# One list of other work for all heads of the attention, and new planning figures

## The chip, the cores and the metric

One core of one Trainium2 chip runs the kernel. The metric is the device time of one execution in microseconds (us). Before the change three runs took 1665.37 to 1666.42 us, the median is 1666.23 us. One further execution was profiled.

## The reference

A block of two branches over a sequence of 1024 tokens of 1024 channels, all in float32:

```python
h = rmsnorm(x, norm_g); proj = h @ w_in      # split in 12 parts
# branch a: mLSTM in both directions, 4 heads of 256, y_a
dq = apply_rope(b_q, positions); dk = apply_rope(b_k, positions)   # 8 heads x 2 x 64
p = softmax(q . k * scale)                   # for both halves j = 0, 1 of a head
att = (p[:, :, 0] - lam * p[:, :, 1]) @ v    # v: 8 heads of 128
y_b = rmsnorm(att, subln_g) * (1 - lambda_init) * silu(b_z)
mix = sigmoid(g_a + gb[0]) * (y_a @ w_branch_a) + sigmoid(g_b + gb[1]) * (y_b @ w_branch_b)
out = rmsnorm(x + mix @ w_out, final_g)
```

The change lies in branch b, the differential attention.

## The kernel before

**Precision.** Every float32 product is made of three matmuls on operands split in a high and a low part (`H` and `L` in the tile names), so each 128-deep step of a projection is three matmuls.

**Stages.** The kernel runs, in this order: norm and transposition of x; most projections of branch a in a form that saves products; the attention of branch b (the stage that the change touches); the mLSTM of branch a; the products with the branch weights and with w_out. Projections that the attention itself needs, or that fill its gaps, run inside the attention stage.

**One head of the attention** works on eight tiles t of 128 rows of q, in units that `da_parts` (L1168) makes:

- S(t): the scores of a tile, both halves of the head, into two PSUM tiles of 128 x 1024 (12 matmuls, L1185). VectorE takes the maximum of each (`nm`, L1188), ScalarE the exponential (`e`, L1190), and VectorE joins both (L1196).
- T(t, g): eight transpositions of the joined tile in two groups of four (L160), each group in a PSUM tile with the tag "T". ScalarE copies it to `pH` (L1209), VectorE makes the low part `pL` (L1210). There are two such PSUM tiles.
- PV(t2, g): the products with v for two tiles t, in two units of 12 matmuls (L1221); ScalarE copies the result to `att` (L1223).
- M(t2): transposition of `att` and the sums of squares of it (L1233); the last one of a head starts the root on GpSimd.
- G(half): scaling, and the store of y_b for a half of the sequence.

`da_cycle` (L1270) puts these into one order per tile: in even tiles S and T of the tile before, then M; in odd tiles S and PV, then T; in tiles 4 and 5 also G of the head before. T, M and G of a head's last tiles fall into the first tiles of the next head.

**The other work** is woven between: rotated q and k of a later head (`da_proj`: four times eight pieces of three matmuls of 512 columns, then the rotation on VectorE and GpSimd and a DMA into place), z of a head (two times eight pieces), v of two heads (`da_v`: 32 pieces of six matmuls of 256 columns, L675), and gates of the final mix (`gate_units`, 16 pieces, taken by `fill(m)`). The even heads in `R_EARLY` have q and k made in an earlier stage and only load them (`load_qk`), and the heads in `Z_EARLY` load z; these units have cost 0. All pieces of `proj` have the line L653.

**The planner.** `Weaver` (L70) sets the order of the matmul engine before anything runs. Each unit has a cost in us (multiples of `MM` and `TP`), names of units after which it may come, each with a lag, and maybe a PSUM tag whose tiles are held for a time after the unit (`LAG`: T tiles 2.9, S 5.0). `weave` takes several lists. A list falls into lanes, each kept in order. At each step the unit goes first that can start first by these figures, and among equals the one whose place in its list, as a share of the list's cost, is lowest:

```python
best = min(heads, key=lambda l: (max(self.ready(l[0][1]), self.now), l[0][0]))
```

A `Chain` is a run of units that is put as a whole once none of them has to wait. The order is kept on the matmul engine; the order on the other engines is made from it later. Weights of a piece are loaded by `run` (L610) up to two keys ahead, on the queue of SyncE, which also carries the loads of q, k and z and the stores of y_b.

**The order before.** `build` weaves head by head: the units of head h with a list of other work for that head, so that each head's list is spread over that head alone. Even heads have a rotated q/k projection and z (48 pieces), odd heads v (32 pieces), head 0 the last 12 pieces of v of heads 0 and 1, a projection and a gate unit, and head 7 a gate unit and z. The units of v for heads 2n and 2n+1 come after the last PV of head 2n-2, which stands in tile 1 of head 2n-1; the halves of z come after G of the head before plus 6.0 us.

Of the kernel before, what the change touches and what calls it, by code (L numbers as in the profile page):

```python
# [13 lines left out]

S = 1024
D = 1024
EPS = 1e-6
NH_A, DH = 4, 256
NH_B = 8
# [15 lines left out]


INF = 1.0e9
FILL = (1, 0, 0, 0, 0, 0, 0, 1)
Z_EARLY = (0, 1, 3, 5)
R_EARLY = (0, 2, 4, 6)  # L40
MM = 0.214
TP = 0.109

LAG = dict(Th=2.9, Sh=5.0, PVh=2.9, Mh=2.0, qk=14.0, T=6.8, PV=3.0, M=1.5, F=6.0, TTh=1.9, TT=3.2, POh=1.6,
# [85 lines left out]
class Block:  # L130
# [529 lines left out]
    def v_units(self, seg, n, done, after=(), order=(0, 1, 2, 3)):  # L660

        box = {}

        def piece(s2, g):
            if g == 0:
                box["ps"] = self.psA.tile([128, 2, 256], F32, name="pj", tag="pj", bufs=2)
            ps = box["ps"]
            i, kh, k0 = g // 4, (g // 2) % 2, 2 * (g % 2)
            wH, wL = (wide(x) for x in self.wt[(seg, n, kh)])
            s = 2 * s2 + i  # L670
            c = slice((s % 4) * 128, (s % 4) * 128 + 128)
            for k in range(k0, k0 + 2):
                hH, hL = (x[s // 4][:, 4 * kh + k, c] for x in (self.hH, self.hL))
                for m, (l, r) in enumerate(((hH, wH), (hL, wH), (hH, wL))):
                    self.t.matmul(ps[:, i, :], lhsT=l, rhs=r[:, k, :], start=(kh == 0 and k == 0 and m == 0),  # L675
                                  stop=(kh == 1 and k == 3 and m == 2))
            if g == 7:
                done(s2, ps)

        return [Unit(6 * TP, lambda s2=s2, g=g: piece(s2, g), ((seg, n, (g // 2) % 2),), after=after)  # L680
                for s2 in order for g in range(8)]

    def bank(self, tag, shape=(128, 512)):
# [397 lines left out]
    def da_proj(self, h, st):  # L1081
        A, v, a, p, q = self.A, self.v, self.a, self.p, self.q
        w1 = self.w1
        fb = lambda x: x.bitcast(F32)
        kA, kB = ("rope", h, 0), ("rope", h, 1)

        def first(half, pa):
            c = slice(half * 512, (half + 1) * 512)
            m = [w1.tile([128, 512], F32, name=f"m{i}", tag=f"m{i}", bufs=1) for i in range(2)]
            st["m"] = m  # L1090
            v.tensor_tensor(out=m[0], in0=pa, in1=self.cosT[:, c], op=ALU.mult)
            v.tensor_tensor(out=m[1], in0=pa, in1=self.sinT[:, c], op=ALU.mult)

        def second(half, pb):
            c = slice(half * 512, (half + 1) * 512)
            if half == 0:
                st["k"] = w1.tile([128, 2, S], F32R, name="kst", tag="kst", bufs=2)
            qq = st["q", half] = w1.tile([128, 2, 512], F32R, name="qq", tag="qq", bufs=3)
            m = st["m"]

            hl = w1.tile([128, 4, 512], F32R, name="hl", tag="hl", bufs=2)
            v.tensor_tensor(out=fb(hl[:, 2]), in0=pb, in1=self.sinT[:, c], op=ALU.mult)
            v.tensor_tensor(out=fb(hl[:, 3]), in0=pb, in1=self.cosT[:, c], op=ALU.mult)
            p.tensor_tensor(out=m[0], in0=m[0], in1=fb(hl[:, 2]), op=ALU.subtract)
            p.tensor_tensor(out=m[1], in0=fb(hl[:, 3]), in1=m[1], op=ALU.add)
            for i in range(2):
                p.tensor_copy(hl[:, i, :], m[i])
                p.tensor_tensor(out=hl[:, 2 + i, :], in0=m[i], in1=fb(hl[:, i, :]), op=ALU.subtract)
            for x in range(2):
                for i, to in enumerate((st["k"][:, :, c], qq)):  # L1110
                    for j in range(2):
                        r, g = 64 * j + 32 * x, 64 * (1 - i) + 32 * j
                        q.dma_start(out=fb(to[r:r + 32]), in_=fb(hl[g:g + 32, x::2]))

        kz = ("w_in", OFF["bz"] + 128 * h)

        def zz(half, ps):
            st["g", half] = g = w1.tile([128, 512], F32, name="zg", tag="zg", bufs=2)
            a.activation(out=g, in_=ps, func=AF.Tanh, scale=0.5)
            v.scalar_tensor_tensor(out=g, in0=g, scalar=1.0, in1=ps, op0=ALU.add, op1=ALU.mult)  # L1120

        def load_qk(half):
            if half == 0:
                st["k"] = w1.tile([128, 2, S], F32R, name="kst", tag="kst", bufs=2)
            st["q", half] = w1.tile([128, 2, 512], F32R, name="qq", tag="qq", bufs=3)
            for x in range(2):
                for j in range(2):
                    r, g = 64 * j + 32 * x, 32 * j
                    if half == 0:
                        q.dma_start(out=fb(st["k"][r:r + 32]), in_=self.rd[h][64 + g:96 + g, x])  # L1130
                    q.dma_start(out=fb(st["q", half][r:r + 32]), in_=self.rd[h][g:g + 32, x, :, half * 512:half * 512 + 512])

        qk = []
        if h in R_EARLY:
            qk = [Unit(0.0, lambda: load_qk(0)), Unit(0.0, lambda: load_qk(1), name=("qk", h), after=((("S", h - 1, 3), 1.0),), lane=1)]
        for half in range(0 if h in R_EARLY else 2):
            qk += self.proj(kA, half, lambda ps, half=half: first(half, ps))
            qk += self.proj(kB, half, lambda ps, half=half: second(half, ps), name=("qk", h))
        def load(half):
            t = w1.tile([128, 512], F32, name="zr", tag="zr", bufs=2)  # L1140
            q.dma_start(out=t, in_=self.zd[h][:, half * 512:(half + 1) * 512])
            zz(half, t)

        if h in Z_EARLY:
            z = [Unit(0.0, lambda half=half: load(half), name=("z", h) if half else None) for half in range(2)]
        else:
            z = self.proj(kz, 0, lambda ps: zz(0, ps)) + self.proj(kz, 1, lambda ps: zz(1, ps), name=("z", h))
        for half in range(2):
            z[(half + 1) * len(z) // 2 - 1].after = ((("G", h - 1, half), LAG["G"]),)
        return qk, z  # L1150
# [17 lines left out]
    def da_parts(self, h, st):  # L1168
# [43 lines left out]
        def pv(t2, g):  # L1212
            vH, vL = st["v"]
            if g == 0:
                st["pv"] = self.bank("T")
            ps = st["pv"]
            pH, pL = st.pop(("pT", t2, g))
            for i in range(4):
                k = 4 * g + i
                for m, (l, r) in enumerate(((vH, pH), (vH, pL), (vL, pH))):  # L1220
                    self.t.matmul(ps[:, 0:256], lhsT=l[:, k, :], rhs=r[:, i, :], start=(k == 0 and m == 0), stop=(k == 7 and m == 2))  # L1221
            if g == 1:
                a.copy(st["att"][:, t2 * 256:(t2 + 1) * 256], ps[:, 0:256])  # L1223
# [24 lines left out]
        def scale(half):  # L1248
# [3 lines left out]
            for i in range(4):  # L1252
# [3 lines left out]
            q.dma_start(out=self.yb[h][:, half * 512:(half + 1) * 512], in_=g)  # L1256

        return dict(
            S=lambda t: Unit(6 * MM, lambda: scores(t), tag="S", hold=LAG["Sh"], name=("S", h, t), after=((("qk", h), 5.0 if h in R_EARLY else LAG["qk"]),)),
            T=lambda t, g: Unit(4 * TP, lambda: transposes(t, g), tag="T", hold=LAG["Th"], name=("T", h, t, g),  # L1260
                                after=((("S", h, t), LAG["T"]),)),
            PV=lambda t2, g: Unit(12 * TP, lambda: pv(t2, g), tag="T" if g == 0 else None, hold=LAG["PVh"], name=("PV", h, t2, g),
                                  after=((("T", h, 2 * t2 + 1, g), LAG["PV"]), (("v", h // 2), 1.0))),
            M=lambda t2: Unit(2 * TP, lambda: squares(t2), tag="T", hold=LAG["Mh"], name=("M", h, t2),
                              after=((("PV", h, t2, 1), LAG["M"]), (("z", h if t2 == 3 else -1), 0.0))),
# [474 lines left out]
    def build(self):  # L1740
# [19 lines left out]
        do = lambda f, cost=0.0: Unit(cost, f)  # L1760
        pool = lambda *x, **k: tc.tile_pool(*x, **k)
        with pool(name="const", bufs=1) as self.const, \
# [112 lines left out]
            w.banks.update(S=1, T=2)  # L1875
            qk, z = zip(*[self.da_proj(h, sts[h]) for h in range(NH_B)])
            v0 = self.da_v(0, sts[0:2])
            w.add(do(lambda: setattr(self, "ahead", True)), *qk[0], *z[0], *v0[:20])
            prev = None
            for h in range(NH_B):  # L1880
                cur = self.da_parts(h, sts[h])
                main = sum((self.da_cycle(cur, prev, t) for t in range(8)), [])
                ahead = qk[h + 1] if h + 1 < NH_B else []
                if h + 1 == NH_B:
                    nxt = fill(FILL[h]) + z[h]
                elif h % 2 == 1:
                    nxt = ahead + self.da_v((h + 1) // 2, sts[h + 1:h + 3]) + fill(FILL[h])
                else:
                    nxt = z[h - 1] + ahead + fill(FILL[h]) + z[h] if h else v0[20:] + ahead + fill(FILL[0])
                w.weave(main, nxt)  # L1890
                prev = cur
            end = sum((self.da_cycle(None, prev, t) for t in range(6)), [])
            w.weave(end[:-2], fill(2))
            more, c = fill(1), self.PIECES // 2
# [85 lines left out]
```

## Time and profile before

| what | us |
|---|---|
| median of three runs | 1666.23 |
| lowest and highest run | 1665.37, 1666.42 |
| profiled execution, its own time | 1662.69 |
| span in the profile | 1660.9 |
| TensorE matmul busy | 1612.8 (97%) |
| VectorE busy | 1076.5 (65%) |
| ScalarE busy | 809.4 (49%) |
| GpSimd busy | 663.1 (40%) |

The span runs from the first to the last instruction of the core. In the profile PE is the matmul engine, PEld its weight loads, DVE VectorE, ACT ScalarE, POOL GpSimd, SP the queue of SyncE. L with a number is a line of the kernel. Tiles are named output<-inputs: S are scores, T the small PSUM tiles, pj the PSUM tiles of projections. A row of the chain of waits has the start, the length, the engine, the tile, the line and the count of instructions. Matmuls are pipelined and their ends are modelled, so a row's length is a little more than the time to the next start.

### The profile page before, as it was taken

The page shows a single profiled execution, that of the slowest core. Times are in us where ns is not written, and L with a number is a line of the kernel's source. Part 1 is how long each engine was busy: PE and PEld are TensorE (multiplying, and loading weights), DVE is VectorE, ACT ScalarE, POOL GpSimd, SP SyncE. Part 2 cuts the span into 40 slices and gives each one's busy share as a digit, 9 for nine tenths or more (in the row PEclk, how much of TensorE's full clock was granted, in tenths as well). Part 3 has the DMA queues.
Part 4 walks back from the last instruction along what each step waited for, and adds up shares of the span by engine and source line. Part 5 has one row for each costly group of instructions (what it writes and reads, how often), then busy time and mean ns, then how long its engine had stood idle before and what let it go on. Part 6 is the DMA issues. An engine that isn't in the chain of part 4 may idle for free.

```text
span 1660.9 us, 25336 instructions
## 1 busy us (share of the span) xinstructions
PE 1612.8 (97%) x9251; PEld 1357.6 (82%) x9251; DVE 1076.5 (65%) x1898; ACT 809.4 (49%) x1634; POOL 663.1 (40%) x709
## 2 busy tenths in 40 slices
PE   7999999999999999999999999999999999999998
PEld 5898778878888888797797887877888888888887
DVE  5734887686876517677768778776157867446633
ACT  6433555555544435555545555554357656442221
POOL 3744676767679722513312511521322332222000
PEclk9999999999999999999999999999999999999999
DMA  5433444444444451511401411310697863466422
GB/s 188 146 127 129 129 129 141 123 132 127 140 122 157 152 165 52 127 41 50 114 20 58 101 40 52 82 47 33 178 316 255 272 201 130 140 229 215 178 90 88
DMA packets 195854, 216.53 MB, mean 130 GB/s; under 512 B 12441, under 2 KB 143858, under 8 KB 195218
## 3 DMA queue, kind: packets, MB, share of 16 engines
q1 hardware_dynamic: 192514, 209.14, 40.8%
q10 hardware_dynamic: 3216, 5.78, 0.9%
q8 instruction: 73, 1.20, 0.3%
q14 instruction: 51, 0.42, 0.1%
HBM read 137.18 MB, written 69.30 MB: 124 GB/s over the span
## 4 chain that ended last, share of the span: by engine, by line
PE 62%; DVE 5%; ACT 4%; POOL 4%; issue 2%; DMA 1%; SPq 0%; POOLq 0%; DVEq 0%; ACTq 0%
PE pj L653 22%; PE T L401 10%; PE S L1185 5%; PE pj L675 5%; PE pj L1690 5%; PE T L160 5%; PE T L1221 5%; ACT e L1190 2%; PE I L156 2%; PE T L156 1%; DVE nm L1188 1%; PE SS L156 1%; PE PO L156 1%; POOL wH L374 1%; POOL s L351 1%
## 5 line engine op out<-in xcount | busy, mean ns | idle before, releaser
L653 PE MATMUL pj<-hH,wH 128*128 128x512 f32 x544 | 222.8, 409 | 0.1
L653 PE MATMUL pj<-hH,wL 128*128 128x512 f32 x544 | 213.9, 393 | 0.8 <-POOL wL L245 0.8
L653 PE MATMUL pj<-hL,wH 128*128 128x512 f32 x544 | 213.2, 392 | 0.6 <-DVE hL L809 0.6
L1190 ACT ACTIVATE e<-S,nm 128x1024 f32<-128x1024 f32 x128 | 142.7, 1122 | 91.0 <-DVE nm L1188 91.0
L1188 DVE TENSOR_REDUCE nm<-S 128x1 f32<-128x1024 f32 x128 | 150.7, 1219 | 46.9 <-PE S L1185 46.7
L247 POOL TENSOR_TENSOR wL<-raw,wH 128x1024 fp32r<-128x1024 f32 x27 | 68.4, 2534 | 149.8 <-ACT wH L239 137.4
L1209 ACT CAST pH<-T 128x512 fp32r<-128x512 f32 x128 | 69.9, 589 | 117.6 <-PE T L160 117.6
L401 PE MATMUL T<-TH,wL 128*128 128x512 f32 x368 | 122.2, 393 | 2.3 <-ACT u L408 2.3
L401 PE MATMUL T<-TH,wH 128*128 128x512 f32 x368 | 122.1, 391 | 0.4 <-ACT u L408 0.3
L653 PEld LDWEIGHTS pj<-hH,wL 128*128 128x128 f32 x544 | 102.1, 188 | 24.2 <-POOL wL L245 2.1
L653 PEld LDWEIGHTS pj<-hL,wH 128*128 128x128 f32 x544 | 102.6, 189 | 17.7 <-DVE hL L809 1.5
L653 PEld LDWEIGHTS pj<-hH,wH 128*128 128x128 f32 x544 | 102.5, 188 | 16.4 <-ACT hH L808 0.5
L1185 PE MATMUL S<-kst,qq 64*128 64x512 f32 x768 | 110.4, 410 | 0.9 <-ACT e L1190 0.6
L1210 DVE TENSOR_TENSOR pL<-T,pH 128x512 fp32r<-128x512 f32 x128 | 82.4, 682 | 29.0 <-ACT pH L1209 29.0
L1185 PEld LDWEIGHTS S<-kst,qq 64*128 64x128 f32 x768 | 69.1, 185 | 31.6 <-issue 12.7
L1245 POOL TENSOR_TENSOR zg<-att,zg 128x512 f32<-128x512 f32 x16 | 21.1, 1316 | 181.4 <-ACT att L1223 165.5
L1196 DVE SCALAR_TENSOR_TENSOR e<-e,r,e 128x1024 f32<-128x1024 f32 x64 | 91.6, 1431 | 2.0
L401 PE MATMUL T<-hH,wH 128*128 128x512 f32 x280 | 92.3, 390 | 0.2 <-DVE cin L578 0.2
L401 PE MATMUL T<-hH,wL 128*128 128x512 f32 x272 | 90.2, 391 | 0.7 <-DVE oz L510 0.7
L597 DVE SCALAR_TENSOR_TENSOR pj<-cin,cols,pj 128x512 f32<-128x512 f32 x128 | 87.1, 747 | 0.0
L401 PEld LDWEIGHTS T<-TH,wL 128*128 128x128 f32 x368 | 69.1, 188 | 20.3 <-ACT u L408 6.1
L401 PEld LDWEIGHTS T<-TH,wH 128*128 128x128 f32 x368 | 69.1, 188 | 15.6 <-ACT u L408 1.2
(417 smaller groups left out, 4596.6 us busy)
## 6 DMA issues: line engine op xcount, KB each, us to landing
raw<-in_w_in_dram SPq DMA_DIRECT2D x76, 512.0 KB, 4.0
rd<-rot SPq DMA_DIRECT2D x16, 512.0 KB, 3.1
x<-in_x_dram SPq DMA_DIRECT2D x8, 512.0 KB, 4.7
avH<-tz SPq DMA_DIRECT2D x16, 256.0 KB, 2.0
cak<-y SPq DMA_DIRECT2D x16, 256.0 KB, 2.7
cakH<-cin SPq DMA_DIRECT2D x16, 256.0 KB, 4.7
cakL<-tz SPq DMA_DIRECT2D x16, 256.0 KB, 4.6
gm<-oz SPq DMA_DIRECT2D x16, 256.0 KB, 2.7
```

The source lines that it names most:

```text
L156: self.t.matmul(out, lhsT=l, rhs=r, start=(i == 0), stop=(i == n - 1))
L160: self.t.transpose(out, in_, self.ident[0:k, 0:k])
L401: self.t.matmul(ps, lhsT=l[:, k, :], rhs=r[:, k, :], start=(first and k == 0 and m == 0), stop=(k == 3 and m == 2), skip_group_check=not f ...
L597: v.scalar_tensor_tensor(out=acc, in0=raw[:, o + x:o + x + 512], scalar=w(x), in1=acc, op0=ALU.mult, op1=ALU.add)
L653: self.t.matmul(ps, lhsT=l[:, k, :], rhs=r, start=(n == 0), stop=(n == 23))
L675: self.t.matmul(ps[:, i, :], lhsT=l, rhs=r[:, k, :], start=(kh == 0 and k == 0 and m == 0), stop=(kh == 1 and k == 3 and m == 2))
L1185: self.t.matmul(ps[:, o], lhsT=qq[r, x, c], rhs=k[r, y, o], start=(m == 0), stop=(m == 2))
L1188: v.tensor_reduce(out=nm, in_=ps, axis=AX.X, op=ALU.max, negate=True)
L1190: a.activation(out=e, in_=ps, func=AF.Exp, bias=nm[:, 0:1], accum_out=Z[:, j, t:t + 1])
L1196: v.scalar_tensor_tensor(out=e0, in0=e, scalar=r[:, 0:1], in1=e0, op0=ALU.mult, op1=ALU.add)
L1221: self.t.matmul(ps[:, 0:256], lhsT=l[:, k, :], rhs=r[:, i, :], start=(k == 0 and m == 0), stop=(k == 7 and m == 2))
L1690: self.t.matmul(ps, lhsT=x[:, s], rhs=y[:, c], start=(k == 0 and m == 0), stop=(k == 7 and m == 2))
```

## The change

The eight weaves become one. All heads' units stand in one main list, and all other work in one second list, which is woven against it from the first tile of head 0 to the last of head 7. All 32 pieces of v of heads 0 and 1 run before the weave (20 before). The second list has, in order: q/k of head 1, the loads of q/k of head 2, a gate unit, the loads of z of head 1; then for h = 2, 4, 6: v of heads h and h+1, q/k of head h+1, z of head h, and the loads of q/k of head h+2 and of z of head h+1 (after head 6: a gate unit and z of head 7). The order of the matmul pieces in it is that of before. The loads of z get a lane of their own, and the first load of q/k of an even head goes to the lane of the second and waits for the scores of the head two before. `FILL` is gone. The planning figures change: `MM` 0.214 to 0.227, S 6 to 7.5 `MM`, a half of PV 12 to 13 `TP`, a piece of v 6 to 6.6 `TP`. The arithmetic of the kernel is the same.

```diff
-FILL = (1, 0, 0, 0, 0, 0, 0, 1)
 Z_EARLY = (0, 1, 3, 5)
 R_EARLY = (0, 2, 4, 6)
-MM = 0.214
+MM = 0.227
 TP = 0.109
...
-        return [Unit(6 * TP, lambda s2=s2, g=g: piece(s2, g), ((seg, n, (g // 2) % 2),), after=after)
+        return [Unit(6.6 * TP, lambda s2=s2, g=g: piece(s2, g), ((seg, n, (g // 2) % 2),), after=after)
                 for s2 in order for g in range(8)]
...
         if h in R_EARLY:
-            qk = [Unit(0.0, lambda: load_qk(0)), Unit(0.0, lambda: load_qk(1), name=("qk", h), after=((("S", h - 1, 3), 1.0),), lane=1)]
+            qk = [Unit(0.0, lambda: load_qk(0), after=((("S", h - 2, 7), 1.0),), lane=1),
+                  Unit(0.0, lambda: load_qk(1), name=("qk", h), after=((("S", h - 1, 3), 1.0),), lane=1)]
...
         if h in Z_EARLY:
-            z = [Unit(0.0, lambda half=half: load(half), name=("z", h) if half else None) for half in range(2)]
+            z = [Unit(0.0, lambda half=half: load(half), name=("z", h) if half else None, lane=2) for half in range(2)]
...
-            S=lambda t: Unit(6 * MM, lambda: scores(t), tag="S", hold=LAG["Sh"], ...
+            S=lambda t: Unit(7.5 * MM, lambda: scores(t), tag="S", hold=LAG["Sh"], ...
...
-            PV=lambda t2, g: Unit(12 * TP, lambda: pv(t2, g), tag="T" if g == 0 else None, ...
+            PV=lambda t2, g: Unit(13 * TP, lambda: pv(t2, g), tag="T" if g == 0 else None, ...
...
-            w.add(do(lambda: setattr(self, "ahead", True)), *qk[0], *z[0], *v0[:20])
-            prev = None
-            for h in range(NH_B):
-                cur = self.da_parts(h, sts[h])
-                main = sum((self.da_cycle(cur, prev, t) for t in range(8)), [])
-                ahead = qk[h + 1] if h + 1 < NH_B else []
-                if h + 1 == NH_B:
-                    nxt = fill(FILL[h]) + z[h]
-                elif h % 2 == 1:
-                    nxt = ahead + self.da_v((h + 1) // 2, sts[h + 1:h + 3]) + fill(FILL[h])
-                else:
-                    nxt = z[h - 1] + ahead + fill(FILL[h]) + z[h] if h else v0[20:] + ahead + fill(FILL[0])
-                w.weave(main, nxt)
-                prev = cur
+            w.add(do(lambda: setattr(self, "ahead", True)), *qk[0], *z[0], *v0)
+            parts = [self.da_parts(h, sts[h]) for h in range(NH_B)]
+            main = sum((self.da_cycle(x, y, t) for x, y in zip(parts, [None] + parts) for t in range(8)), [])
+            prev, nxt = parts[-1], qk[1] + qk[2] + fill(1) + z[1]
+            for h in (2, 4, 6):
+                nxt += self.da_v(h // 2, sts[h:h + 2]) + qk[h + 1] + z[h] + (qk[h + 2] + z[h + 1] if h < 6 else fill(1) + z[7])
+            w.weave(main, nxt)
```

More of the change, by code (lines that the diff above doesn't have):

```diff
@@ L1258, in da_parts @@
         return dict(
-            S=lambda t: Unit(6 * MM, lambda: scores(t), tag="S", hold=LAG["Sh"], name=("S", h, t), after=((("qk", h), 5.0 if h in R_EARLY else LAG["qk"]),)),
+            S=lambda t: Unit(7.5 * MM, lambda: scores(t), tag="S", hold=LAG["Sh"], name=("S", h, t), after=((("qk", h), 5.0 if h in R_EARLY else LAG["qk"]),)),
             T=lambda t, g: Unit(4 * TP, lambda: transposes(t, g), tag="T", hold=LAG["Th"], name=("T", h, t, g),
                                 after=((("S", h, t), LAG["T"]),)),
-            PV=lambda t2, g: Unit(12 * TP, lambda: pv(t2, g), tag="T" if g == 0 else None, hold=LAG["PVh"], name=("PV", h, t2, g),
+            PV=lambda t2, g: Unit(13 * TP, lambda: pv(t2, g), tag="T" if g == 0 else None, hold=LAG["PVh"], name=("PV", h, t2, g),
                                   after=((("T", h, 2 * t2 + 1, g), LAG["PV"]), (("v", h // 2), 1.0))),
```

## The prediction

> **What bounds the kernel now.** I read the page's busy line first, then busy time by stretches of the attention stage, then the chain of waits inside single stretches.
>
> ```profile
> span 1660.9 us, 25336 instructions
> ...
> PE 1612.8 (97%) x9251; PEld 1357.6 (82%) x9251; DVE 1076.5 (65%) x1898; ACT 809.4 (49%) x1634; POOL 663.1 (40%) x709
> ```
>
> The matmul engine is busy 97% of the span, so only what it waits can be won. The change acts in the attention stage alone. Its first and last scores matmul mark it, and the longest wait of the engine there is for the pL tiles (sum, times, longest):
>
> ```profile
> L1185 PE MATMUL S<-kst,qq x768: 383/393/628, 621.2 to 1143.1; 64*128 64x512 f32 x192
> PE T L160 <- DVE pL L1210: 12.5, 7, 2.2
> ```
>
> The stage by stretches, cut where the matmul engine's idle time begins and ends (columns: length, then busy time of PE, PEld, DVE, ACT, POOL, then granted clock):
>
> ```profile
> 702.00:743.00 41.00, 41.00 (x340) 38.31 (x339) 30.03 (x43) 21.36 (x48) 6.32 (x10) 1.00 0.15 44
> 743.00:757.00 14.00, 11.63 (x85) 9.37 (x84) 11.27 (x17) 10.72 (x24) 5.70 (x5) 1.00 0.44 132
> 757.00:818.00 61.00, 61.00 (x372) 48.71 (x370) 46.22 (x63) 30.01 (x65) 23.68 (x24) 1.00 0.25 61
> 818.00:833.00 15.00, 12.21 (x82) 9.15 (x83) 12.44 (x17) 9.16 (x21) 2.98 (x4) 0.92 0.47 107
> 833.00:876.00 43.00, 43.00 (x353) 40.31 (x352) 28.57 (x42) 21.25 (x48) 6.77 (x10) 0.99 0.10 31
> 1121.00:1127.00 6.00, 3.89 (x32) 2.80 (x30) 4.86 (x8) 4.02 (x10) 0.00 (x0) 1.00 0.00 0
> ```
>
> Inside a head the engine idles not at all (41.00 of 41, 61.00 of 61, 43.00 of 43). The idle time lies at the seams around the odd heads and in tile 4 of head 7 (1121 to 1127), 2 to 3 us at a time. The chain shows why. First a stretch of head 1, filled with pieces of the v projection (six matmuls each), one tile of scores (S) to the next:
>
> ```profile
> 710.80 1.59 PE S L1185 x11
> 712.39 1.02 PE T L160 x8
> 713.41 2.86 PE pj L675 x24
> 716.27 0.22 PE T L160 x2
> 716.49 1.42 PE pj L675 x12
> 717.92 1.59 PE S L1185 x12
> 719.51 3.02 PE T L1221 x24
> 722.53 1.43 PE pj L675 x12
> 723.96 0.87 PE T L160 x8
> 724.83 1.42 PE pj L675 x12
> 726.26 1.59 PE S L1185 x12
> ```
>
> Even tile: S, transpositions, 4 pieces, squares, 2 pieces. Odd tile: S, the products with v, 2 pieces, transpositions, 2 pieces. Now head 2, filled with the three-matmul pieces of `proj`, with the starts of tiles 4, 5 and 6:
>
> ```profile
> 773.59 1.58 PE S L1185 x12
> 775.17 1.02 PE T L160 x8
> 776.20 2.75 PE pj L653 x12
> 778.95 0.22 PE T L160 x2
> 779.17 2.09 PE pj L653 x9
> 781.26 1.60 PE S L1185 x11
> ...
> 789.43 1.58 PE S L1185 x12
> ...
> 796.84 1.59 PE S L1185 x12
> ...
> 810.31 1.58 PE S L1185 x11
> ```
>
> Here the even tile has 4 + 3 pieces. And the seam before head 3, with no piece at all:
>
> ```profile
> 817.97 1.64 PE S L1185 x11
> 819.61 1.23 DVE nm L1188
> ...
> 826.22 2.26 DVE nm L1188 x2
> 828.48 0.61 DVE pL L1210
> 829.13 0.44 PE T L160 x2
> 829.57 0.76 PE S L1185 x2
> ```
>
> The squares need the PSUM bank that pL frees. VectorE comes to pL only after both maxima (2.26 us): pieces normally hide this, and here there are none.
>
> **The change part by part.** What matters is how many pieces the planner wants, and how many it has.
>
> *The planning figures.* Scores go from 1.28 to 1.70 us (measured 1.59), a `proj` piece from 0.642 to 0.681 (measured 2.09/3 = 0.70), a v piece from 0.654 to 0.719 (1.43/2 = 0.72), products with v from 1.31 to 1.42 a half (3.02/2 = 1.51). None changes an instruction; they change how many pieces the planner puts before a unit is ready by its LAG figures. Even tile: the squares need a T bank, 2.9 - 0.436 = 2.46 us after the transpositions, 4 pieces before and after. The next S is due 5.0 us after the last: 0.87 + 4 x 0.642 + 0.22 = 3.66 left 1.34, so 3 pieces; now 0.87 + 2.72 + 0.22 = 3.81 leaves 1.19, so 2. Odd tile: 2 + 2 in both. Tile 4 takes 6. In tile 5 the scale unit's bank is held 2.46 us more, so 4 + 2. A head wants 6+4+6+4+6+6+6+4 = 42 pieces; head 0, with no head before it, 8+7+7+4+6+4+6+4 = 46.
>
> *One list.* It holds four rotated q/k projections (32 pieces each), four of z (16), three of v (32) and two gate units (16): 320, or 40 a head. Demand by lags (42) lies above the share (40), so the lags place the pieces and other work runs a little ahead. One block is left: v of heads 2n and 2n+1 waits for the last products of head 2n-2, in tile 1 of an odd head. Ahead of the first block stand 32 + 16 = 48 pieces, of which head 0 takes 46; between blocks 32 + 32 + 16 = 80 against 84. So tile 0 of heads 1, 3 and 5 has 2 pieces of 6, where it had none. Gone are the empty tiles 6 and 7 of heads 1, 3 and 5, tile 7 of heads 2, 4 and 6, and tile 4 of head 7. The end of head 7 stays: z of head 7 waits for the scale units of head 6, which leaves 3 pieces in tile 6 and none in tile 7, as now.
>
> *The stage in tiles.* Two more places are needed: tile 0 of head 1 with its successor, empty of pieces, and tile 6 of head 7.
>
> ```profile
> 693.14 1.60 PE S L1185 x11
> ...
> 698.78 1.66 PE S L1185 x11
> 1136.28 1.59 PE S L1185 x11
> ```
>
> An even tile takes 781.26 - 773.59 = 7.67 now, less one piece 6.97. An odd one takes 789.43 - 781.26 = 8.17, tile 4 takes 796.84 - 789.43 = 7.41. Tile 5 takes 810.31 - 796.84 = 13.47 with 11 pieces, 10.0 without five of them; I take 10.1. A full head is 3 x 6.97 + 3 x 8.17 + 7.41 + 10.1 = 62.9. In heads 1, 3 and 5, tile 0 stays at the 698.78 - 693.14 = 5.6 of the empty one, since pL ends it and two pieces only fill part of the wait; five tiles with v pieces take 0.15 more each (717.92 - 710.80 = 7.12 against 6.97): 62.9 - 6.97 + 5.6 + 0.75 = 62.3. Head 0 starts with S (1.6), 0.85 of transpositions from tile 1 on, and 8, 7 and 7 pieces of 0.70: 7.2, 7.4 and 7.4; then come 8.17 x 3 + 6.97 x 2: 60.4. Head 7 up to its last tile: 2 x 6.97 + 2 x 8.17 + 7.41 + 10.1 + 5.0 (1143.1 - 1.8 - 1136.28) = 52.8. Sum 60.4 + 3 x 62.9 + 3 x 62.3 + 52.8 = 488.8. Now it is 1143.1 - 621.2 = 521.9, less 1.8 within the last S (1.6 and a short wait): 520.1.
>
> *v of heads 0 and 1 ahead of the loop.* The last 12 pieces move from head 0 to before the first S: 12 x 0.72 = 8.6 us, the same on both sides, as the engine has no gap there. So the stage wins 520.1 - 488.8 - 8.6 = 22.7.
>
> *Lanes and loads.* The first half of q and k of an even head (four DMAs for k, four for q) is now held until the scores of the head two before are done; its buffers are free only then, so nothing becomes later. The z loads of heads 1, 3 and 5 (one DMA, one tanh, one VectorE operation per half) get a lane of their own and come up to half a head earlier. I cost both at nothing: inside a head VectorE is busy 46.22 of 61 us, 76%, and shorter heads take that to some 80%. Without that cover they would stand ahead of a pL: two operations on 128x512 as pL is, 0.61 each by its row, for two halves of three heads 7 us at most.
>
> *What the rows can't show.* All engines but the matmul engine are put in a new order around the new places. From below it costs nothing (the v stretches run with these piece counts and idle 0). From above it is the first rival's 15.9. I take 4.7, near the lower end because those rows are nearest: some 0.6 us a head. So 22.7 - 4.7 = 18 us.
>
> The profiled execution took 1662.7 us, a span of 1660.9 and 1.8 around it, and goes to 1644.7. The median of the runs, 1666.2, lies 3.5 above it; the same step gives **1648**.
>
> The seam at 818 to 833 has a granted clock of 0.92, about 1.2 us; the other stretches have 0.99 or 1.00. I leave it in both sums. The Trainium skill (TensorE: Matmul & The Clock Gate, "HAM oscillation — how this bites in real kernels") says that an idle gap over some 3.4 us throttles the array; by that rule the shorter seams would win this 1.2 us too.
>
> **The rivals.**
>
> *Ten pieces are too few between `proj` pieces.* They are a little shorter than v pieces, and the even tile now leaves S 0.7 us less. If the old 7.67 us are needed, each of some 23 even tiles outside the v stretches waits 0.69: 15.9 us, a gain of 22.7 - 15.9 = 6.8, 1659. For it: VectorE is the next busiest. Against: v stretches have 7.12 (717.92 - 710.80) and idle 0.
>
> *The seams can't be filled.* If the waits on pL come from two T banks and not from missing pieces, they only move with the seams: no change, 1666. Against: the same two banks idle 0 in every body. The Trainium skill (Perfetto Trace Analysis, "Optimization Strategy") speaks for it: a gap that repeats can mean too few PSUM buffers. By it the gaps would be found between the seams too, and the trace has none there.
>
> *Shares decide after all*, 40 pieces a head without the lag's excess: tile 0 of heads 1, 3 and 5 is then full. Its 5.6 us hold 6.97 - 4 x 0.69 = 4.2 of work now, so 3 x 1.4 come back, and the 4.7: 1648 - 8.9 = 1639.
>
> *Slower: a weight late behind the load queue.*
>
> ```profile
> SPq L1131 <- PE S L1185: 75.2, 3, 28.6
> ```
>
> The queue stands up to 28.6 us at the loads of q, which wait for scores. Today the seam lies between the end of v and the next rotated projection; now it follows at once. Its second weight is needed 8 pieces (about 12 us) after v ends. If its raw columns stood behind such a wait, each of three places would lose up to 16.6 us, 50 in all: 1666.2 - 22.7 + 50 = 1693. It decides from a weight 12 + 22.7/3 = 20 us late. Against: the queue waits there today too, in an odd head without new raw loads.
>
> **How the numbers follow.** Forecast 0.67; too few pieces 0.12; no change 0.07; shares 0.08; slower 0.06. The forecast's own range is 1642 to 1656: the sum without the 4.7 and the clock's 1.2, and with 8 us more, half the first rival's price. To leave out no more than 2 in 10 the range takes in most of the shares and of the first rival: 1640 to 1662. What can be told from no change is 0.2%, 3.3 us. Faster: 0.67 + 0.08 + 0.11 = 0.86; same 0.07; slower 0.07.
>
> **What would show it.** Right: head to head 62 to 63 us instead of 520.1/8 = 65; no idle time in tiles 6 and 7 of heads 1, 3 and 5; some 1.4 us still lost in their tile 0; pieces 4 + 2 in even tiles of `proj`; the end of head 7 as now. Wrong: idle inside the bodies, ahead of the transpositions or of S (first rival); seams as long as now elsewhere (second); the engine waiting for wL at the first pieces after v (fourth).

## The result, and the profile after

Three runs of the changed kernel took 1644.37 to 1645.83 us, median **1645.74**, against 1666.23 before: a ratio of 0.9876 (95% interval 0.9853 to 0.9898). The forecast was 1648, inside 1640 to 1662. The profiled execution took 1645.74 us too.

Line numbers up to about 1130 are lower by one now (`proj` L652, `v` L674, the transpositions L159); from 1185 on they are the old ones. The page's span and busy line after:

```profile
span 1643.9 us, 25333 instructions
...
PE 1610.4 (98%) x9251; PEld 1356.5 (83%) x9251; DVE 1085.3 (66%) x1898; ACT 808.1 (49%) x1634; POOL 665.4 (40%) x709
```

The matmul engine does the same work in a span 17.0 us shorter. The scores' group after (times, then first and last start) bounds the stage:

```profile
L1185 PE MATMUL S<-kst,qq x768: 383/393/502, 630.3 to 1122.0; 64*128 64x512 f32 x192
```

Less the same 1.8 us inside the last S, first S to last S is 1122.0 - 1.8 - 630.3 = 489.9 us, where it was 520.1 and 488.8 was forecast. What the engine still waits for from 630 to 1122 (sum, times, longest):

```profile
PE T L159 <- DVE pL L1210: 0.6, 1, 0.6
PE T L159 <- DVE e L1196: 0.3, 1, 0.3
PE S L1185 <- ACT e L1190: 0.2, 1, 0.2
```

The 12.5 us of waits for pL have gone down to 0.6, and the six waits for `att` (5.1 us before) are gone. The stretches that were cut for before, now over the changed kernel (length, then PE, PEld, DVE, ACT, POOL busy, then the clock):

```profile
702.00:743.00 41.00, 41.00 (x338) 37.63 (x338) 33.16 (x46) 22.82 (x52) 6.26 (x10) 1.00 0.12 39
743.00:757.00 14.00, 14.00 (x105) 12.02 (x105) 9.83 (x16) 8.73 (x20) 5.61 (x5) 1.00 0.32 86
757.00:818.00 61.00, 61.00 (x385) 49.35 (x385) 50.52 (x66) 32.39 (x70) 25.08 (x26) 1.00 0.34 85
818.00:833.00 15.00, 14.96 (x109) 12.22 (x106) 12.31 (x16) 9.02 (x20) 4.17 (x3) 1.00 0.18 37
833.00:876.00 43.00, 43.00 (x353) 39.63 (x352) 33.84 (x48) 25.93 (x59) 8.33 (x13) 1.00 0.18 53
1121.00:1127.00 6.00, 4.84 (x40) 4.06 (x37) 4.66 (x7) 4.40 (x12) 2.85 (x3) 1.00 0.15 35
```

Inside the heads the engine still idles not at all, with the new order on all other engines; the seams at 743 and 818 are full, and the clock is 1.00 in each. Only the end of head 7 has a hole. The chain of waits over tile 0 of head 2, with the first S of tiles 1 and 2:

```profile
753.98 1.58 PE S L1185 x12
755.57 1.02 PE T L159 x8
756.59 2.74 PE pj L652 x12
759.33 0.22 PE T L159 x2
759.54 1.39 PE pj L652 x6
760.94 1.59 PE S L1185 x10
...
769.18 1.59 PE S L1185 x12
```

The same view over tile 0 of head 3, the seam that was empty:

```profile
817.06 1.58 PE S L1185 x12
818.64 1.02 PE T L159 x8
819.67 2.06 PE pj L652 x9
821.72 0.40 PE T L159 x2
```

The even tile holds 4 + 2 pieces and takes 760.94 - 753.98 = 6.96 us, the odd one 769.18 - 760.94 = 8.24. Tile 0 of head 3 holds 9 matmuls, three pieces, where it had none. Head 2 takes 817.06 - 753.98 = 63.1.

**What was given back.** The stage wins 520.1 - 489.9 = 30.2, and 8.6 of v ahead of it come off: 21.6 net. The span wins 17.0. The largest part of the difference lies where nothing was expected, in the products with the branch weights (mix stage). There the engine has a wait of which the trace of before has no row:

```profile
PE pj L652 <- DVE tga L1632: 2.7, 3, 1.6
```

The chain around the first of the three:

```profile
1510.26 7.74 DMA yraw<-in_w_out_dram
1518.00 0.02 issue
1518.02 0.63 ACT sl_wo L1660
1518.65 0.02 issue
1518.67 1.29 DVE sl_wo L1661 x2
1519.97 0.61 DVE tga L1632
```

VectorE stands at the low part of a w_out row, which waits for the row's load; behind it on VectorE is `tga`, which frees a PSUM tile. Step by step between the two traces, matmul by matmul, these places cost 3.2 us. The three loads are woven with `w.weave(loads, passA[k + 1:-k])` (L1929 before): they lie at shares 0, 1/3 and 2/3 of their list, and in the other list two units of cost 0 lie at 1/3 and 2/3 too, but for rounding. Which goes first is decided by the last bit of sums of `3 * MM`. With 0.214 the loads stand ahead of pieces 0, 36 and 68, with 0.227 ahead of 0, 34 and 70.

### The profile page after: what moved, and what is told of

Same layout as the page of the kernel before. It is cut to its first block, busy times and chain, and to the rows that moved or that the text cites. A ratio compares the mean times of both kernels' runs of the same rounds, so it can differ in the third digit from the quotient of the medians.

```text
span 1643.9 us, 25333 instructions
## 1 busy us (share of the span) xinstructions
PE 1610.4 (98%) x9251; PEld 1356.5 (83%) x9251; DVE 1085.3 (66%) x1898; ACT 808.1 (49%) x1634; POOL 665.4 (40%) x709
## 4 chain that ended last, share of the span: by engine, by line
PE 60%; DVE 5%; POOL 4%; DMA 3%; ACT 3%; issue 2%; SPq 0%; POOLq 0%; DVEq 0%; ACTq 0%
PE pj L652 18%; PE T L400 10%; PE S L1185 6%; PE T L1221 6%; PE pj L1690 5%; PE T L159 5%; PE pj L674 5%; PE I L155 2%; PE T L155 2%; DMA bm<-bd 1%; PE SS L155 1%; PE PO L155 1%; POOL wH L373 1%; ACT e L1190 1%; POOL s L350 1%
## 5 line engine op out<-in xcount | busy, mean ns | idle before, releaser
L652 PE MATMUL pj<-hH,wH 128*128 128x512 f32 x544 | 223.6, 411 | 0.1
L652 PE MATMUL pj<-hH,wL 128*128 128x512 f32 x544 | 213.7, 393 | 0.8 <-POOL wL L244 0.8
L652 PE MATMUL pj<-hL,wH 128*128 128x512 f32 x544 | 213.0, 392 | 0.6 <-DVE hL L808 0.6
L652 PEld LDWEIGHTS pj<-hH,wL 128*128 128x128 f32 x544 | 102.1, 188 | 24.3 <-POOL wL L244 2.1
L652 PEld LDWEIGHTS pj<-hL,wH 128*128 128x128 f32 x544 | 102.7, 189 | 17.1 <-DVE hL L808 1.5
L652 PEld LDWEIGHTS pj<-hH,wH 128*128 128x128 f32 x544 | 102.5, 189 | 16.2 <-ACT hH L807 0.5
L1196 DVE SCALAR_TENSOR_TENSOR e<-e,r,e 128x1024 f32<-128x1024 f32 x64 | 98.7, 1542 | 2.0
L652 PE MATMUL pj<-sl_yb,wH 128*128 128x512 f32 x256 | 79.3, 391 | 2.7 <-DVE tga L1632 2.7
```

Of the source, the lines that this page charges most:

```text
L652: self.t.matmul(ps, lhsT=l[:, k, :], rhs=r, start=(n == 0), stop=(n == 23))
L1196: v.scalar_tensor_tensor(out=e0, in0=e, scalar=r[:, 0:1], in1=e0, op0=ALU.mult, op1=ALU.add)
```

## The experiments

The kernels ran in three groups (after_again, tie, flip, vfree; figures, list, zlane, v0; tie_again, mm, vfig, full), each with its own runs of the kernel before beside it (medians 1665.34, 1665.43 and 1667.16 us); the ratios go by those. Medians in us:

| run | what it is | median | ratio to before (95%) |
|---|---|---|---|
| after_again | the change | 1644.61 | 0.9873 (0.9858 to 0.9887) |
| tie | the change, w_out loads as before | 1641.32 | 0.9851 (0.9835 to 0.9868) |
| tie_again | tie once more | 1640.84 | 0.9849 (0.9836 to 0.9863) |
| flip | before, w_out loads as after | 1669.79 | 1.0024 (1.0015 to 1.0033) |
| v0 | before, v of heads 0, 1 ahead | 1666.30 | 1.0005 (0.9996 to 1.0015) |
| figures | before, four new figures | 1664.94 | 0.9990 (0.9980 to 1.0001) |
| list | tie, four old figures | 1660.90 | 0.9977 (0.9961 to 0.9992) |
| mm | list, new MM | 1652.85 | 0.9921 (0.9907 to 0.9935) |
| vfig | list, new v price | 1650.50 | 0.9912 (0.9895 to 0.9928) |
| zlane | tie, z loads in the common lane | 1683.26 | 1.0112 (1.0097 to 1.0127) |
| vfree | tie, seven v pieces earlier | 1647.27 | 0.9891 (0.9876 to 0.9906) |
| full | tie, four v pieces earlier, dearer v | 1644.40 | 0.9869 (0.9855 to 0.9882) |

### The loss in the mix stage: after_again, tie, flip

> The changed kernel as it is, on the chip of the other three, as their measure. Expected 1645.7 us, 20.5 below the kernel before, with three waits of the matmul engine for tga in the mix stage, 3.2 us by the steps between the two traces.

In `tie` the loads are put by hand where the kernel before has them; in `flip` the kernel before gets the places 34 and 70 by the same edit:

```diff
-            w.weave(loads, passA[k + 1:-k])
+            mixed = passA[k + 1:-k]
+            w.add(loads[0], *mixed[:36], loads[1], *mixed[36:68], loads[2], *mixed[68:])
```

> The changed kernel, but the three loads of w_out rows stand by hand where the kernel before has them (ahead of pieces 0, 36 and 68 of the mix stage's list, instead of 0, 34 and 70); the attention is untouched. Theory (the new MM moved these loads across their neighbours in the list, and a late load costs the mix stage 3.2 us): 3.2 us below the changed kernel, 1642.5, and no wait for tga. Rival (the mix stage loses because it begins earlier or in another state behind the shorter attention, whatever the loads' order): within 1 us of the changed kernel, the waits remain.

> The kernel before, with only these three loads put where the changed kernel has them (ahead of pieces 0, 34 and 70); the attention is untouched. Theory (order of the loads): 3.2 us above the kernel before, 1669.4, with the same three waits for tga. Rival (shorter attention): within 1 us of the kernel before.

`tie` is 1644.61 - 1641.32 = 3.3 us faster than the change, and its waits have no row for `tga`. `after_again` was expected to show three such waits and has two, 1.8 us in all in its profiled execution, so the length of the waits varies from one execution to the next. `flip` is 0.24% (0.15 to 0.33), 2.5 to 5.5 us, slower than before, and has the row:

```profile
PE pj L653 <- DVE tga L1632: 2.4, 3, 1.3
```

The theory holds in both directions: with the old attention as with the new one, the order of three loads decides on these 3 us. The rival (a mix stage that suffers from the shorter attention) falls. `tie` is the fastest kernel of the study, 1.5% below before.

### List and figures alone: figures, list, v0

`figures` is the kernel before with the lines of the four prices changed, and the w_out loads put by hand where it has them. `list` is `tie` with those four as before:

```diff
-MM = 0.227
+MM = 0.214
-        return [Unit(6.6 * TP, lambda s2=s2, g=g: piece(s2, g), ((seg, n, (g // 2) % 2),), after=after)
+        return [Unit(6 * TP, lambda s2=s2, g=g: piece(s2, g), ((seg, n, (g // 2) % 2),), after=after)
```

and likewise `6 * MM` for S and `12 * TP` for PV.

> The kernel before with the four new planning figures alone: one list for each head, no new lanes, v of heads 0 and 1 as before, the loads of w_out rows where the kernel before has them. Heads keep their 34 and 46 pieces; by the planned order only single pieces move (2 instead of 1 in tile 6 of the odd heads, 1 instead of 0 in tile 7 of heads 2 and 4 and in tile 4 of head 7), the seams stay. Theory (the gain comes from where the list has pieces, so from the list): some 4 us below the kernel before (six to seven pieces of 0.7 us laid into idle tiles), 1662. Rival (the measured figures make the gain): more than half of it, under 1655.

> The changed kernel's one list, its lanes and its v of heads 0 and 1 ahead, but with the four planning figures of before (and the loads of w_out rows where the kernel before has them). By the planned order even tiles hold 7 pieces instead of 6, tile 0 of heads 1, 3 and 5 none instead of 2, 3 and 3, tile 4 of head 7 none instead of 6. Theory (list): against run tie 8 pieces of 0.7 us are missing in tiles 0 (5.8 us) and 6 in tile 4 of head 7, which shortens it by 1.7 (2.6 us): 8.4 us above run tie, 1649.7, that is 15 to 16 us below the kernel before. Rival (figures): within 4 us of the kernel before.

`v0` is the kernel before with `*v0` instead of `*v0[:20]` ahead of the loop and without `v0[20:]` in head 0.

> The kernel before, with the last 12 pieces of v of heads 0 and 1 moved ahead of the first scores, and nothing else. By the planned order head 0 then has 48 pieces instead of 60 and all else stays. Expected by the sum: the first scores 8.6 us later, head 0 8.6 us shorter, the time within 1.5 us of the kernel before. If the move itself costs or brings something (pieces in head 0 that hide waits, or a wait of the first scores), the time goes by more than 1.5 us.

`v0` came out as reckoned: its first S starts at 630.4 as in the changed kernel, and the time is that of before (-0.04 to +0.15%). The other two missed. `figures` brings 0 to 0.2%, not 4 us. `list` brings under a third of what was expected, 4.5 us, and its attention, with v ahead of it, ends no earlier than before in the profiled execution (1663.48 us, 2.6 above the median of its runs). The scores' group of `list`:

```profile
L1185 PE MATMUL S<-kst,qq x768: 383/393/793, 630.3 to 1143.8; 64*128 64x512 f32 x192
```

Last S at 1143.8, where before had 1143.1. Alone each part brings next to nothing, together they bring 24. Neither theory covers that: the list needs the figures. The trace of `list` shows a wait of ScalarE that the attention of `tie` has not (sum, times, longest):

```profile
ACT wH L238 <- DMA raw<-in_w_in_dram: 10.7, 3, 3.6
```

The chain in tile 7 of head 1 of `list`:

```profile
750.07 2.38 POOL wL L224
752.45 0.02 issue
752.46 3.46 DMA raw<-in_w_in_dram
755.93 0.02 issue
755.95 1.05 ACT wH L238
757.00 2.20 ACT e L1190 x4
759.20 0.27 ACT att L1223
759.47 0.04 issue
759.51 0.66 PE T L159 x4
```

The raw columns of the next weight are loaded when GpSimd has freed a raw buffer (`wL`). The cast to `wH` stands at the head of ScalarE's queue and waits; behind it are four parts of the exponentials and the copy to `att`, for which the matmul engine waits. In `tie` the same cast stands behind the exponentials of that tile (ScalarE in order of time: start, length, operation; the row between the two casts is the first exponential of tile 7):

```profile
745.14 1.13 ACT L223 CAST wH<-raw 128x512 fp32r<-128x512 f32 x2
748.74 1.12 ACT L1190 ACTIVATE e<-S,nm 128x1024 f32<-128x1024 f32 x1 [2.47 <-DVE nm L1188]
...
751.50 1.07 ACT L238 CAST wH<-raw 128x1024 fp32r<-128x1024 f32 x1
```

There it waits for nothing.

### Two costs apart: mm, vfig

The orders that the planner makes show which figure does what. New prices for S and PV change not one place on any engine once MM and the v price are new. MM sets the 6 or 7 pieces in even tiles, and so whether tile 0 of heads 1, 3 and 5 has pieces. The v price sets 5 or 6 pieces in tile 4 of an odd head, and so the place of that cast. So `mm` is `list` with MM = 0.227 alone, and `vfig` is `list` with 6.6 * TP for a v piece alone.

> The kernel of run tie once more, as the measure of the other three beside it. Expected 1641.3.

> Run list with one of the four new figures: MM. By the planned order even tiles then hold 6 pieces and tile 0 of heads 1, 3 and 5 holds 2, as in run tie; but in tile 7 of these heads the third weight cast (raw columns to the high part, on ScalarE) stands ahead of the exponentials, as in run list, where it waits for its load 10.7 us in three times. Theory (a weight late behind its raw buffer holds the exponentials; run list lost 2.1 to 2.9 us by it in each of three tiles): 6.5 to 8 us above run tie, 1648 to 1649, with ScalarE waiting for raw columns in three places. Rival (the empty tile 0 is what makes run list slow): within 1 us of run tie.

> Run list with another one of the four: the price of a v piece. By the planned order even tiles hold 7 pieces, tile 0 of heads 1, 3 and 5 none and tile 4 of head 7 one, as in run list; but tile 4 of the odd heads holds 5 instead of 6, and by this the third weight cast stands behind the exponentials, as in run tie. Theory (empty tiles and late weight are two separate costs): no wait of ScalarE for raw columns, and some 8 us above run tie for the missing pieces, 1649, up to 3 more where the clock is lowered behind an empty tile. Rival (the late weight is all that run list lost): within 2 us of run tie.

`mm` lies 12.0 us above `tie_again`, and ScalarE waits in three places:

```profile
ACT wH L238 <- DMA raw<-in_w_in_dram: 11.2, 3, 3.8
```

The mechanism is as expected. From S to S, tile 7 of heads 1, 3 and 5 takes 11.1, 10.5 and 12.2 us, in `tie` 8.3: 9.0 together. Tile 0 of head 2 takes 1.1 longer behind the first, and tile 0 of heads 3 and 5 lacks a piece, which costs 0.7 each: 11.5 of the 12.0. But not all of this is the wait for the weight. Behind it the granted clock (third number from the end) falls in heads 1 and 5 and not in head 3:

```profile
757.00:760.00 3.00, 3.00 (x17) 2.16 (x17) 0.51 (x2) 0.00 (x0) 0.00 (x0) 0.62 0.18 61
886.00:889.00 3.00, 3.00 (x24) 2.38 (x24) 2.03 (x4) 0.73 (x2) 0.00 (x0) 1.00 0.35 124
1013.00:1016.00 3.00, 3.00 (x12) 2.09 (x12) 1.83 (x3) 0.58 (x1) 0.69 (x1) 0.62 0.64 178
```

Where the clock held, the late weight cost 10.5 - 8.3 = 2.2 us; three times that is 6.6, inside the 6.5 to 8 expected. The low clock cost some 1.7 us more behind each of the other two, which the expectation had left out.

`vfig` lies 9.7 us above `tie_again`, with no wait of ScalarE for raw columns in the stage; the matmul engine waits for pL as it did before the change:

```profile
PE T L159 <- DVE pL L1210: 8.3, 5, 2.0
```

The fastest of its runs, 1648.19, lies 7.8 us above the fastest of `tie_again`: that is the 8 us of missing pieces. The profiled execution is the slowest of the six, 1657.13, and in it tile 1 of heads 1, 3 and 5 takes 11.8 us each with the four pieces that take 8.9 in `tie`, at a lowered clock (last section). That the clock makes the rest of the 9.7 in the median too is argued from this one execution. Both costs are real and nearly add up: 12.0 + 9.7 = 21.7, where `list`, which has both, lies 1660.90 - 1641.32 = 19.6 above `tie`. It is this sum that the two new figures remove.

### The lane of the z loads: zlane

```diff
-            z = [Unit(0.0, lambda half=half: load(half), name=("z", h) if half else None, lane=2) for half in range(2)]
+            z = [Unit(0.0, lambda half=half: load(half), name=("z", h) if half else None) for half in range(2)]
```

> The kernel of run tie with the z loads of heads 1, 3 and 5 back in the common lane of the list. A z load waits in the planner for the products of the head before, and the pieces of v stand behind it: by the planned order tiles 1 to 5 of the odd heads hold no piece and tile 6 holds 21 to 23. Theory (a lane of their own is what lets one list run at all): each odd head loses some 6.8 us (25 pieces of 0.72 gone from tiles that shorten by 11.2 only), 20 us above run tie, 1662. Rival (lanes cost and bring nothing, as I put them into the sum): within 2 us of run tie.

42 us above `tie`, twice what was expected and slower than before. The waits for pL in the stage:

```profile
PE T L159 <- DVE pL L1210: 17.1, 13, 2.2
```

The expectation took tiles without a piece to shorten by 11.2 us an odd head. Tiles 1 to 5 of head 1 shortened from 41.4 to 35.1, by 6.3: tile 3 took 8.34 us with four pieces and with none. The rest of the 42 us is not taken apart. A lane that costs nothing is what keeps the list moving at all.

### Filling tile 0 of the odd heads: vfree, full

Only the eighth piece of v brings a tile that needs the buffer of the head before; the planner makes all of them wait. `vfree` frees the first seven of them, `full` the first four, with 7.2 * TP for a v piece beside it.

```diff
         un = self.v_units("bv", n, done, ((("PV", 2 * n - 2, 3, 1), 0.0),))
+        for u in un[:7]:
+            u.after = ()
```

> The kernel of run tie, and the first seven pieces of each v projection no longer wait in the planner for the last products of the head before (only the eighth, which brings the first v tile, does). By the planned order tile 0 of heads 1 and 3 then holds 6 pieces, that of head 5 still 3. Theory (tile 0 of an odd head loses about 1.4 us for want of pieces): 2 x 1.4 = 2.8 us below run tie, 1639.7, and no idle time at the starts of heads 1 and 3. Rival (pL comes late there whatever stands ahead of it, from the two T banks): within 0.5 us of run tie, the idle time remains or is found one tile later.

> The kernel of run tie; the first four pieces of each v projection no longer wait in the planner for the last products of the head before, and a v piece is planned at 7.2 instead of 6.6 transpositions. By the planned order tile 0 of heads 1, 3 and 5 then holds 6 pieces, the other tiles of the v stretches one piece less, tile 6 of head 7 six instead of three, and no weight cast stands ahead of exponentials that its load would hold. Theory (1.4 us lost in tile 0 of three heads, some 1 us at the end of head 7 for want of pieces, and the late weight was what made run vfree slow): 3 to 5 us below run tie, 1637 to 1638. Rival (five and three pieces are too few between the tiles of a v stretch): about 0.7 us lost in each of some 18 tiles, 12 us above that, slower than run tie.

Both missed on the whole and hit on the spot. In `vfree` tiles 0 and 1 of head 1, with four pieces more (4 x 0.72 = 2.87 us), take 707.68 - 692.27 = 15.41, in `tie` 706.22 - 692.28 = 13.94: 1.4 us are won, as the prediction put it. But the list holds no more pieces than it did. The seven that stand earlier are missing in tiles 3 and 4 of head 7, and the weight cast came ahead of the exponentials in heads 1, 3 and 5 again (6.1 us in three waits). So `vfree` is 6.0 slower than `tie`. `full` mended the end of head 7. Tiles 2 and 6 of its odd heads 1, 3 and 5 hold five v pieces. Four of these six tiles lose nothing: they take 6.40 us, the 7.12 of six pieces less one. Tile 6 of heads 3 and 5, where an operation on z (`zg`) stands on VectorE ahead of pL, takes 7.61 and 7.12. So its rival, a loss in each of some 18 tiles, falls. It met another late load, k of head 5 in the chain:

```profile
941.11 2.40 DMA kst<-hl
```

Tile 0 of head 5 took 11.1 us instead of 7.1: the waits for k make 1.7 of it, the granted clock behind them (0.78 in 944 to 946, 0.50 in 946 to 948, 0.87 in 948 to 950) as much again. Around head 6 a weight was late once more (2.9 us). `full` is 3.6 above `tie_again`. Filling the last 1.4 us of three tiles was not reached. It would take an order in which no load gets nearer to its use, and none was tried that did.

## Why the prediction was right or wrong

**What bounds the kernel, and where.** Right: the engine's idle time lay at the seams, and pieces of other work filled them.

**The pieces.** Even heads got 6 4 6 4 6 6 6 4, head 0 got 8 7 7 4 6 4 6 4, head 7 three in tile 6 and none in tile 7, all as worked out. Tile 0 of heads 1, 3 and 5 got 2, 3 and 3 where 2 were said, as tile 4 of an odd head holds five v pieces and not six. That the lags place the pieces and not the shares is right; the third rival falls with it. Tile 0 of the odd heads takes 5.1 us and not 5.6, and the tile after it 8.9 and not 8.3: the row that the 5.6 was read from (698.78, x11) leaves out the first matmul of its S, which started at 698.15. The two tiles together came out as said.

**The stage in tiles.** 488.8 forecast, 489.9 measured. Even heads 63.1 (62.9), odd ones 61.9 to 62.2 (62.3). Head 0 took 61.8 and not 60.4: tile 2 took 8.4 instead of 7.4, with two short waits, and three odd tiles 0.1 more each. v ahead of the loop cost its 8.6 and nothing else, as `v0` shows by itself; the first S comes 9.1 us later, and the other 0.5 lies ahead of the v pieces.

**Lanes and loads.** Costed at nothing, and they cost nothing: VectorE is busy 50.52 of 61 us in head 2 (83%, some 80% were said), and no z operation came ahead of a pL that the matmul engine needed. What the sum did not ask is what the lane is for: without it the kernel is slower than before (`zlane`).

**The planning figures.** The step named four and reckoned their effect on even and odd tiles together with the list. It missed that two of them (S and PV) change nothing here, and that the v price, by one piece in tile 4, decides where a weight cast falls on ScalarE. Without it the gain would have been 12 us smaller, as `mm` shows, and the sum would have come out the same: the pieces that the prediction worked out, two in tile 0 and six in tile 4 of the odd heads, are those of `mm`. That the changed kernel has five there, and escapes the late weight, was luck.

**"The change acts in the attention stage alone"** is the step that failed. MM prices the mix stage too. There it tipped a tie of shares and cost 3.3 us by `tie`, 2.5 to 5.5 by `flip`. The prediction priced what the figures do to the attention and asked for no other list that uses MM.

**What the rows can't show (4.7).** Put in the wrong place. The new order of all other engines cost 1.1 us in the attention (489.9 - 488.8), near the lower bound of nothing. Outside of it 3.2 went to the mix stage and some 1.4 to small steps at the start and after the attention that are not explained further (0.5 of it before the first v piece). In the profiled execution these sizes nearly cancel, which is luck: 1644.7 forecast, 1645.74 measured, and -4.7 + 1.1 + 3.2 + 1.4 = 1.0.

**The 3.5 us between the profiled execution and the median.** Carried over, and wrong: after the change both are 1645.74. This accounts for the forecast of 1648 being 2.3 too high. A cause that fits is the clock. In the 51 later runs of the kernel before the granted clock lies between 0.993 and 0.998, and the time goes with it: 1662.65 to 1664.21 us at 0.998, the clock of the profiled execution, and 1668.3 to 1668.5 at 0.993. The changed kernel has 0.998 or 0.999 in each run. The three runs behind the 1666.23 have no clock on record, so that it makes all of the 3.5 is argued, not shown.

**The clock at the seams.** The stretch at 818 to 833 went from 0.92 to 1.00. The prediction says that it left these 1.2 us in both sums, but its 488.8 is added up from tiles at full clock: the sum had them won already, and the low end of the forecast's range counts them twice. The Trainium skill (TensorE: Matmul & The Clock Gate, "HAM oscillation — how this bites in real kernels") was right in direction; its bound on the length of a gap does not fit here, see below.

**The rivals.** *Ten pieces too few*: an even tile of 6.96 us without idle time settles it, and in `full` one piece less costs nothing in four of the six v tiles named above. *The seams can't be filled*: the two T banks are the same and the waits for pL went from 12.5 to 0.6, so the Trainium skill's reading of repeating gaps as missing PSUM buffers (Perfetto Trace Analysis, "Optimization Strategy") does not hold for them. *A weight late behind the load queue*: not in the changed kernel, but one piece away from it. In `list`, `mm` and `vfree` it is there three times. Its price is 2 to 4 us a place, with the clock behind it, not 16.6, and its way is another one: the raw columns wait for a raw buffer that GpSimd frees, and the cast that waits for them holds up the exponentials on ScalarE. Nothing waited for wL at the matmul engine, where the prediction would have looked. A chance of 0.06 was little for a mechanism kept off by one piece.

## What to carry to other kernels

When a planning figure changes, look for every list that uses it, also in stages that the change does not mean: equal shares of a float sum are a tie that any new figure can tip, and an order that matters is written out. Filler work is a fixed stock. Before it is moved into a gap, ask which tile gives it up, and whose loads come nearer to their use: a cast waiting for its load holds everything behind it on its engine. Parts of a change should be run alone and together; here two parts bring 0.5 and 4.5 us alone and 24 together. A wait of the matmul engine can cost more than its length, by the clock behind it: look at the clock in short stretches before a loss is put down to the wait alone.

## What the runs showed of the hardware

The clock is lowered behind waits shorter than the 3.4 us that the prediction spoke of, and not each time. The same wait of 2.02 us in tile 0 of head 1, in before and in `vfig` (start, length, and in brackets the idle time before):

```profile
697.78 0.44 PE L160 MATMUL T<-ident,att 128*128 128x128 f32 x2 [2.02 <-DVE pL L1210]
698.15 2.29 PE L1185 MATMUL S<-kst,qq 64*128 64x512 f32 x12
```

```profile
698.18 0.44 PE L159 MATMUL T<-ident,att 128*128 128x128 f32 x2 [2.02 <-DVE pL L1210]
698.55 3.46 PE L1185 MATMUL S<-kst,qq 64*128 64x512 f32 x12
```

The granted clock of `vfig` there, by stretches (the third number from the end):

```profile
690.00:700.00 10.00, 7.98 (x49) 5.87 (x50) 7.42 (x13) 8.15 (x20) 2.94 (x4) 0.94 0.65 150
700.00:712.00 12.00, 12.00 (x78) 10.42 (x77) 6.23 (x8) 3.78 (x7) 1.29 (x1) 0.77 0.00 1
```

0.77 over 12 us is 2.8 us lost, more than the wait itself, and the matmul engine counts as busy all the while. In before the same place kept 1.00, and the dip came at another seam (0.92 at 818 to 833). In the one profiled execution of `list` a wait of 2.02 us stands in tile 0 of heads 1, 3 and 5, and tile 1 behind it, with four pieces each time, takes 11.8, 10.1 and 8.9 us. The Trainium skill (TensorE: Matmul & The Clock Gate, "HAM oscillation — how this bites in real kernels") speaks of gaps over some 3.4 us; single waits of 2.0 to 2.2 us were enough here, some of the time. In these places transpositions stand on both sides of the wait, so that about 3.5 us pass without another matmul (695.07 to 698.55 in `vfig`); the traces do not show whether that counts. But in `full` a wait of 1.51 us for k in the midst of scores matmuls was followed by 0.50 in 946 to 948. With the seams the dips went, and so did much of the scatter: before took 1662.6 to 1669.3 us in 51 runs, `vfig` with its empty tiles 1648.2 to 1657.1 in six, the changed kernel 1644.1 to 1645.8 in seven and `tie` 1640.4 to 1642.1 in nine.
